# A two-layer encoder trunk with four token mixers: the S5 mixer's steps come first, not last, in the list that interleaves the mixers

## The chip, the cores and the metric

One core of a Trainium2 chip runs the whole program. The metric is device time in microseconds (us) from the start to the end of one execution; the time of the kernel before is the median of three executions. Engines are named as in the profile: PE (TensorE's matmuls), PEld (its weight loads), DVE (VectorE), ACT (ScalarE), POOL (GpSimd) and SP (SyncE, which here only issues DMAs).

## What is computed

The input is one sequence of 512 frames of width 1024, in float32. Each of two layers does this (cut to what matters):

```python
h = x @ w_in[l]                      # projections for four mixers
o_ret = retention(rq, rk, rv, rg)    # branch 0
o_att = chunk_attention(aq, ak, av)  # branch 1
o_gla = gla(gq, gk, gv, gr, ga)      # branch 2
o_s5  = s5(su, ...)                  # branch 3
mixed = sum(sigmoid(x @ w_gate[l, b] + b_gate[l, b]) * (o[b] @ w_branch[l, b]) for b in range(4))
x = layer_norm(ALPHA * x + mixed @ w_out[l])
ffn = (silu(x @ w_ffn_gate[l]) * (x @ w_ffn_up[l])) @ w_ffn_down[l]
x = layer_norm(ALPHA * x + ffn)
```

S5 is a complex diagonal linear recurrence over the 512 frames, 16 groups of 16 channels with 64 states each, followed by a GELU and a sigmoid gate. The four mixers do not depend on each other. Each needs only its own projections of x, and the merge needs all four.

## The kernel before, in words

Every large product is made as three passes in a 32-bit format of PE, on a high and a low half of each operand. The halves of a weight block are made on the chip: ACT casts the block (`wh<-wr`), DVE subtracts (`wl<-wr,wh`). So each 1024x128 block of weights costs PE 48 matmuls of 256 columns, ACT one cast and DVE one subtraction. `wr` has two buffers, `wh` and `wl` three.

A layer has five stages: projections; the stage of the mixers, with the gates between them; the output projection with a layer norm; the FFN's first products; the FFN's last product with a layer norm. Only the mixers' stage concerns us. In it stand, as Python generators that yield between their steps:

- `attention` (tiles `as` scores, `pp` probabilities, `at` transposed, `ao` output), four heads;
- `ret()`, which makes retention's projections (`rq`, `rk`, `rg`) and then runs `retention` (`rs`, `ro`, `rn`), the latter only once one half of attention's output is there;
- `gl()`, which makes GLA's projections (`gn`, `gq`, `gr`) once attention is done, and runs `gla` (`ga`, `gz`, `gu`, `go`) once one half of retention's output is there;
- `s5`, eight steps j = 0 to 7 and a gated end (`sg`). A step has a pair of matmuls for its inputs (`sv<-stk,sbs`), six products on DVE, two scans on DVE (`sm<-mag,sm`), six more products, two splits into halves (`xrh`/`xrl`, `xih`/`xil`), and, one step later, six matmuls that add its part to the output (`sy<-xrh,cpd`). The multiplying tables `er`, `ei` of a step are made on POOL in layer 0 (six operations on 128x512) and loaded by DMA in layer 1. The input `stk` of step j+1 is cast on ACT (`prepare`) after the states of step j;
- `gate_stream`, the filler: 32 gates (`pg`, 48 matmuls each) and 32 branch products (`pb`, 6 matmuls each). At most seven gates may wait for their branch (`CAP`), and a branch product needs the branch's mixer to be done. The order of branches is attention, retention, GLA, S5.

What sets the order is `run`. It keeps a model of each engine's clock (`Pace`: a cost for every operation, a time at which each tile is ready). At every turn it asks each generator, in the order of its list, whether its next step is ready by the model's time of PE, and takes the first that is. If none is, it takes the one that is ready soonest. The filler stands last in that list. S5 yields twice per step with `spare`, which says "not ready before the model's DVE clock is less than 3 us ahead of the model's PE clock":

```python
live = [[g, next(g)] for g in (*gens, fill)]
...
now = [i for i in ok if at[i] <= pace.at["T"]]
i = now[0] if now else min(ok, key=lambda j: at[j])
...
return lambda: max(pace.at["V"] - SPARE, pace.ready(need))
```

The order in which steps are taken is the order in which instructions are written. The tile framework then orders each engine's instructions by a schedule of its own, near to that. Every engine works its list strictly in order at run time. Buffers: 53 slots of 128x512 floats for everything in the stage, and in PSUM five banks for the mixers' tiles and three for gates and branch products.

Of the kernel before, what the change touches and what calls it, by code (L numbers as in the profile page):

```python
# [132 lines left out]
def trunk_kernel(ctx: ExitStack, tc: tile.TileContext, xn, xt, wt, w2, wbr, wo, wgu, wdn,  # L133
# [23 lines left out]
    def slot(s, dt=F32, tag="a"):  # L157
        n = nm(s)
        return ap_.tile([P, 512], dt, tag=tag, name=n, bufs=BUFS[tag])
# [13 lines left out]
    def split(h, l, src):  # L173
        A.copy(h, src)
        V.tensor_tensor(l, src, h.bitcast(F32), ALU.subtract)

    def split_slots(s, src, tags=("a", "a")):
        h, l = slot(s + "h", F32R, tags[0]), slot(s + "l", F32R, tags[1])
        split(h, l, src)
        return h, l  # L180
# [154 lines left out]
    def gemm_t(src, s, late=None):  # L335

        return gemm_ts([src], s, late)[0]
# [16 lines left out]
    def gemm_n(srcs, width, pre=None, late=None):  # L354

        pss = [mm_ps("gn") for _ in range(3)] + [mx_ps("gn")]
        ws = []

        def prod(c, t):
            h, l = ws[c]  # L360
            for kk in range(2):
                k = 2 * c + kk
                for j, (xx, w) in enumerate(((XH, h), (XL, h), (XH, l))):
                    T.matmul(pss[t][:, :width], xx[:, k, P * t:P * t + P],
                             w[:, kk * width:(kk + 1) * width],
                             start=(k == 0 and j == 0), stop=(k == 7 and j == 2))

        for c in range(4):
            ws.append(wload(srcs[c], 2 * width, 2, lambda i: pre(2 * c + i)) if pre else
                      wload(srcs[c], 2 * width))  # L370
            if late and c == 2:
                late()
            for t in range(3 if late and c < 3 else 4):
                prod(c, t)
            if late and c == 2:
                for c_ in range(3):
                    prod(c_, 3)
        return pss
# [108 lines left out]
    def silu_of(ps):  # L487

        t, s = slot("st"), slot("sg")
        A.activation(t, ps, AF.Tanh, scale=0.5)  # L490
        V.scalar_tensor_tensor(s, t, 1.0, ps, ALU.add, ALU.mult)
        return s
# [84 lines left out]
    def rotary(ps, ctab, stab, order):  # L577
        f = slot("rf")
        A.copy(f, ps)
        yield [f, ctab, stab]  # L580
        sw = mx_ps("rs")
        T.matmul(sw, perm, f, start=True, stop=True)
        a, b = slot("ra"), slot("rb")
        V.tensor_tensor(b, sw, stab, ALU.mult)
        V.tensor_tensor(a, f, ctab, ALU.mult)
        V.tensor_tensor(a, a, b, ALU.add)
        return spread(split_slots("rq", a), order)

    def spread(hl, order):

        x = dr.tile([3, P, 512], F32, name=nm("spr"))
        for i in range(3):
            SP.dma_start(x[i], hl[order[i]].bitcast(F32))
        return x
# [75 lines left out]
    def gla_in(pss):  # L670

        gk, gv = slot("gk"), []
        ga = sm.tile([P, 4, 32], F32, tag="ga", name=nm("ga"))
        G.memset(ga[:, :, 16:32], 1.0)
        for t in range(4):
            A.copy(gk[:, P * t:P * t + P], pss[t][:, 0:P])
            A.copy(ga[:, t, 0:16], pss[t][:, 384:400])
            g = slot("gv", F32R)
            split(g[:, 0:256], g[:, 256:512], pss[t][:, 128:384])
            gv.append(g)  # L680
        return gk, ga, gv
# [298 lines left out]
    def run(fill, *gens):  # L980


        live = [[g, next(g)] for g in (*gens, fill)]
        while live:
            at = [pace.ready(x[1]) for x in live]
            ok = [i for i, t in enumerate(at) if t is not None]
            now = [i for i in ok if at[i] <= pace.at["T"]]
            i = now[0] if now else min(ok, key=lambda j: at[j])
            try:
                live[i][1] = next(live[i][0])  # L990
            except StopIteration:
                live.pop(i)
# [9 lines left out]
    for l in range(L):  # L1002
        tt_ = lambda i, s: gemm_t(wt[l, i], s)

        pv = gemm_n(w2[l, 0], 512, load_x if l == 0 else None, rest)
        vr, va = [], []
        for t in range(4):
            for c, v in enumerate((vr, va)):
                x = slot("v", F32R)
                split(x[:, 0:256], x[:, 256:512], pv[t][:, 256 * c:256 * c + 256])  # L1010
                v.append((x[:, 0:256], x[:, 256:512]))
        uspr = []
        for i in range(2):
            ps = tt_(11 + i, "su")
            uspr.append(spread(split_slots("u", ps), (0, 1, 0)))
        if l == 0:
            SP.dma_start(ct, cst)
            SP.dma_start(pt, par)
            G.tensor_scalar(hb, pt[:, :, 0:36], 0.5, None, ALU.mult)
            s5c = s5_constants(0)  # L1020
        aq = [split_slots("aq", tt_(4 + i, "aq")) for i in range(2)]
        ak = [split_slots("ak", tt_(6 + i, "ak")) for i in range(2)]
        if l > 0:
            rows()
            with tc.issue_after(wdma[0].ins):
                for t in range(4):
                    for h in range(2):
                        SP.dma_start(xsp[P * t:P * t + P, 512 * h:512 * h + 512], xh[t][h])
        brs = [[None, None] for _ in range(4)]
        mix = []  # L1030
        rd = {}

        def ret():
            tabs = []
            for i in range(4):
                tabs.append(slot("rot"))
                SP.dma_start(tabs[i], rot[i])
            yield ()
            q = yield from rotary(tt_(0, "rq"), *tabs[0:2], (0, 1, 0))
            yield ()  # L1040
            k = yield from rotary(tt_(1, "rk"), *tabs[2:4], (0, 0, 1))
            g = []
            for i in range(2):
                yield ()
                g.append(silu_of(tt_(2 + i, "rg")))
            yield lambda: None if brs[1][0] is None else 0.0
            yield from retention(q, k, vr, g, brs[0])

        def gl():
            yield lambda: None if brs[1][1] is None else 0.0  # L1050
            kv = gla_in(gemm_n(w2[l, 1], 400))
            yield ()
            gq = slot("gq")
            A.activation(gq, tt_(8, "gq"), AF.Copy, scale=32.0 ** -0.5)
            g = []
            for i in range(2):
                yield ()
                g.append(silu_of(tt_(9 + i, "gr")))
            yield lambda: None if brs[0][0] is None else 0.0
            yield from gla(l, *kv, gq, g, brs[2])  # L1060

        g_gate = gate_stream(l, (1, 0, 2, 3), brs, mix)
        run(g_gate, attention(l, aq, ak, va, brs[1]), ret(), gl(), s5(l, s5c, uspr, brs[3]))
        xh = [[slot("x") for _ in range(2)] for _ in range(4)]
        for t in range(4):
            for h in range(2):
                src = xn if l == 0 else xsp
                SP.dma_start(xh[t][h], src[P * t:P * t + P, 512 * h:512 * h + 512])
        gt, bt = ln_params(l, 0)
        rest, rows = proj_ln(l, 0, [m[0] for m in mix], [m[1] for m in mix], 8, wo[l], 4, 2, xh, gt, bt, False)  # L1070


        gt, bt = ln_params(l, 1)
        ghs, gls = [], []
        ps = gemm_ts([wgu[l, i] for i in range(3)], "pg", rest)
        for f in range(NF):
            if f > 0:
                ps += [gemm_t(wgu[l, i], "pg") for i in range(max(3, 2 * f), 2 * f + 2)]
            pg, pu = ps[2 * f:2 * f + 2]
            if f == 1:  # L1080
                rows()
            s = slot("fs")
            A.activation(s, pg, AF.Silu)
            V.tensor_tensor(s, s, pu, ALU.mult)
            h, l_ = split_slots("g", s, ("acc", "acc") if f < 4 else ("sg", "sg") if f < 7 else ("a", "a"))
            ghs.append(h)
            gls.append(l_)
            if l + 1 < L and f == 0:
                s5c = s5_constants(l + 1)
            if l + 1 < L and f % 2 == 0 and 4 <= f < 20:  # L1090
                j = f // 2 - 2
                for i, x in enumerate(s5_table(j, s5c[3])):
                    SP.dma_start(esp[j, i], x)
        rest, rows = proj_ln(l, 1, ghs, gls, NF, wdn[l], 4, 2, xh, gt, bt, l == L - 1)
# [140 lines left out]
```

## Time and profile before

| | us |
|---|---|
| median of three executions | 1720.33 (1717.82 to 1720.64) |
| the profiled execution's own time | 1720.08 |
| its span, first to last instruction | 1717.9 |
| PE busy | 1651.2 (96%) |
| PE weight loads busy | 1531.0 (89%) |
| DVE busy | 1000.2 (58%) |
| ACT busy | 613.4 (36%) |
| POOL busy | 353.4 (21%) |
| mixers' stage, layer 0 (first `as` to first `pj`) | 63.9 to 453.9 = 390.0 |
| mixers' stage, layer 1 | 927.9 to 1297.4 = 369.5 |

PE is busy nearly always, but "busy" also counts matmuls at half clock; the granted clock beside each window tells how much of that there is (1.00 is 2.4 GHz, and a mean of 0.94 over a window means that 12% of it went at 1.2 GHz). The time that the program could lose or win in a stage is therefore the stage's length against PE's work in it at full clock. DVE's 58% is a mean of very unlike stages; a window for each part of the mixers' stage tells more.

### The profile page before, as it was taken

The page shows a single profiled execution, that of the slowest core. Times are in us where ns is not written, and L with a number is a line of the kernel's source. Part 1 is how long each engine was busy: PE and PEld are TensorE (multiplying, and loading weights), DVE is VectorE, ACT ScalarE, POOL GpSimd, SP SyncE. Part 2 cuts the span into 40 slices and gives each one's busy share as a digit, 9 for nine tenths or more (in the row PEclk, how much of TensorE's full clock was granted, in tenths as well). Part 3 has the DMA queues.
Part 4 walks back from the last instruction along what each step waited for, and adds up shares of the span by engine and source line. Part 5 has one row for each costly group of instructions (what it writes and reads, how often), then busy time and mean ns, then how long its engine had stood idle before and what let it go on. Part 6 is the DMA issues. An engine that isn't in the chain of part 4 may idle for free. (4 is left out here: it accounts for less than half of the span.)

```text
span 1717.9 us, 27806 instructions
## 1 busy us (share of the span) xinstructions
PE 1651.2 (96%) x11596; PEld 1531.0 (89%) x11596; DVE 1000.2 (58%) x1473; ACT 613.4 (36%) x1012; POOL 353.4 (21%) x363
## 2 busy tenths in 40 slices
PE   8999998889999999999999999999999999999997
PEld 7989898779889999988889898988898899999886
DVE  4666579987586533322374665789865833333226
ACT  4454532233343222221154545433342522222112
POOL 0601024560038921000060000122300600000002
PEclk9998999899999999999999999999999999999999
DMA  6532212222433333322327332233324232222232
GB/s 200 176 111 76 86 62 94 82 82 99 141 99 99 123 123 117 119 98 98 111 74 259 104 96 92 64 117 125 125 93 160 86 102 96 99 99 99 98 99 74
DMA packets 66205, 186.94 MB, mean 109 GB/s; under 512 B 7136, under 2 KB 7328, under 8 KB 66080
## 3 DMA queue, kind: packets, MB, share of 16 engines
q1 hardware_dynamic: 66080, 185.17, 32.7%
q8 instruction: 91, 1.49, 0.4%
q14 instruction: 34, 0.28, 0.0%
HBM read 170.46 MB, written 14.68 MB: 108 GB/s over the span
## 5 line engine op out<-in xcount | busy, mean ns | idle before, releaser
L121 DVE TENSOR_TENSOR wl<-wr,wh 128x1024 fp32r<-128x1024 f32 (+2 forms) x250 | 317.3, 1270 | 440.9 <-ACT wh L121 427.0
L121 ACT CAST wh<-wr 128x1024 fp32r<-128x1024 f32 (+2 forms) x250 | 257.5, 1032 | 671.1 <-PE pg L121 223.6
L121 PE MATMUL pg<-XH,wh 128*128 128x256 f32 x2432 | 337.4, 281 | 2.2 <-DVE fs L121 2.2
L121 PE MATMUL pg<-XL,wh 128*128 128x256 f32 x2432 | 333.8, 280 | 2.5 <-DVE XL L121 2.5
L121 PE MATMUL pg<-XH,wl 128*128 128x256 f32 x2432 | 333.0, 280 | 0.0
L121 PEld LDWEIGHTS pg<-XH,wh 128*128 128x128 f32 x2432 | 312.1, 192 | 8.1 <-issue 3.1
L121 PEld LDWEIGHTS pg<-XL,wh 128*128 128x128 f32 x2432 | 306.0, 191 | 3.3 <-DVE XL L121 3.3
L121 PEld LDWEIGHTS pg<-XH,wl 128*128 128x128 f32 x2432 | 305.9, 191 | 0.4
L121 POOL TENSOR_TENSOR rs<-ve,ct 128x1 f32<-128x1 f32 x16 | 10.9, 682 | 718.2 <-DVE ve L121 718.2
L121 DVE TENSOR_TENSOR fs<-fs,pg 128x512 f32<-128x512 f32 x44 | 30.2, 687 | 159.5 <-PE pg L121 159.5
L121 PE MATMUL pj<-wl,gh 128*128 128x512 f32 x320 | 102.3, 393 | 0.0
L121 PE MATMUL pj<-wh,gl 128*128 128x512 f32 x320 | 101.8, 391 | 0.0
L121 PE MATMUL pj<-wh,gh 128*128 128x512 f32 x320 | 101.7, 391 | 0.0
L121 POOL TENSOR_TENSOR acc<-acc,sg 128x512 f32<-128x512 f32 x32 | 61.6, 1929 | 170.3 <-DVE sg L121 170.3
L121 PEld LDWEIGHTS pj<-wh,gh 128*128 128x128 f32 x320 | 59.9, 188 | 13.5
L121 PEld LDWEIGHTS pj<-wl,gh 128*128 128x128 f32 x320 | 60.1, 188 | 13.1
L121 PEld LDWEIGHTS pj<-wh,gl 128*128 128x128 f32 x320 | 60.1, 188 | 12.7
L121 PE MATMUL gn<-wh,XH 128*128 128x400 f32 (+1 forms) x128 | 49.1, 384 | 6.2 <-ACT XH L121 6.2
L121 POOL TENSOR_TENSOR hr<-hv,ct 128x8 f32<-128x8 f32 x8 | 13.2, 1648 | 192.0 <-DVE hv L121 192.0
L121 PE MATMUL pb<-brh,bwh 128*128 128x512 f32 x128 | 51.8, 404 | 0.0
L121 PE MATMUL pb<-brh,bwl 128*128 128x512 f32 x128 | 51.3, 401 | 0.0
L121 PE MATMUL pb<-brl,bwh 128*128 128x512 f32 x128 | 51.3, 401 | 0.0
(320 smaller groups left out, 2584.0 us busy)
## 6 DMA issues: line engine op xcount, KB each, us to landing
wr<-in_wt SPq DMA_DIRECT2D x90, 512.0 KB
wr<-in_wgu SPq DMA_DIRECT2D x88, 512.0 KB
wr<-in_wdn SPq DMA_DIRECT2D x44, 512.0 KB
bwr<-in_wbr SPq DMA_DIRECT2D x32, 256.0 KB
wr<-in_wo SPq DMA_DIRECT2D x16, 512.0 KB
skr<-spr SPq DMA_DIRECT2D x32, 192.0 KB
wr<-in_w2b SPq DMA_DIRECT2D x8, 400.0 KB
wr<-in_w2a SPq DMA_DIRECT2D x8, 256.0 KB
```

Of the source, the lines that this page charges most:

```text
L121: r = fn(out, *a, **kw)
```

## The change: what it does

One line. S5's generator moves from the last to the first place among the four mixers in the list of `run`; the filler still comes last.

```diff
         g_gate = gate_stream(l, (1, 0, 2, 3), brs, mix)
-        run(g_gate, attention(l, aq, ak, va, brs[1]), ret(), gl(), s5(l, s5c, uspr, brs[3]))
+        run(g_gate, s5(l, s5c, uspr, brs[3]), attention(l, aq, ak, va, brs[1]), ret(), gl())
```

No instruction is added or removed; both programs hold the same matmuls, the same DVE, ACT and POOL operations and the same DMAs. What moves is the order on every engine, from the start of the mixers' stage to its end, in both layers.

In the three places that follow, neighbouring rows that only repeat are left out. On PE in layer 0, the second pair of S5's input products (`sv`, the step j = 1). Before, it stands behind GLA's last output products (`go`) and the eleventh gate, 1295 matmuls into the stage:

```order
L121 MATMUL go_2934<-gsh_2858,qh_2324 128x256
L121 MATMUL go_2934<-gsl_2859,qh_2324 128x256
L121 MATMUL go_2934<-gsh_2858,ql_2325 128x256
L121 MATMUL pg_2974<-XH,wl_2970 128x256 x8
L121 MATMUL sv_3029<-stk_2546,sbs_902 128x512
L121 MATMUL sv_3031<-stk_2546,sbs_902 128x512
L121 MATMUL pb_3057<-brh_2275,bwh_2480 128x512
```

With the change it stands 561 matmuls into the stage, between two heads of attention:

```order
L121 MATMUL pg_1653<-XL,wh_1648 128x256 x8
L121 MATMUL pg_1653<-XH,wl_1649 128x256 x8
L121 MATMUL sv_1708<-stk_1563,sbs_794 128x512
L121 MATMUL sv_1710<-stk_1563,sbs_794 128x512
L121 MATMUL ao_1292<-pth_1570,v_271 128x128
L121 MATMUL ao_1292<-ptl_1571,v_271 128x128
L121 MATMUL at_1742<-ct,pp_1380 128x128
```

Steps 1 to 7 thus moved out of the last third of the stage into attention, retention and GLA, and gates that stood ahead of them now stand behind them.

On PE in layer 0, the end of S5. Before, S5's last `sy` group is followed by 4 gates, the 12 `sg` products and 8 branch products up to the first output projection. With the change the last `sy` group (here broken up by a gate) is followed by more than 13 gates and 15 branch products, the first of them still GLA's:

```order
L121 MATMUL pg_3975<-XL,wh_3970 128x256 x4
L121 MATMUL sy_2998<-xrl_3782,cpd_3683 128x512
L121 MATMUL sy_2998<-xih_3785,cpd_3683 128x512
L121 MATMUL sy_2998<-xil_3786,cpd_3683 128x512
L121 MATMUL pg_3975<-XH,wl_3971 128x256 x8
L121 MATMUL pb_4054<-brh_3620,bwh_3679 128x512
L121 MATMUL sg_4026<-ygh_2682,swgh_3895 128x512
L121 MATMUL pg_4141<-XH,wh_4136 128x256 x8
```

What moved here is nearly ten gates and seven branch products, from ahead of S5's last step to behind it.

On ACT in layer 0, the casts around the input of S5's step 7. Before, the cast of the second state half (`xih`) of step 6, the next step's input (`stk`) behind it, and only weights and gates around them:

```order
L121 CAST wh_4547<-wr_4546 128x1024
L121 ACTIVATE sg_4371<-pg_4322,hb 128x512
L121 CAST xih_4293<-sm_4200 128x512
L121 CAST stk_4305<-skr_4208 96x512
L121 CAST cpd_4384<-scc_771 128x2x32
```

With the change the same pair, with GLA's and retention's norms (`hq`), states (`gsh`) and outputs (`brh`) ahead and behind:

```order
L121 CAST gsh_3367<-gs_3354 128x512
L121 CAST brh_3435<-hf_3433 128x512
L121 ACTIVATE hq_3513<-go_3509 128x512
L121 CAST xrh_3586<-sm_3180 128x512
L121 CAST xih_3590<-sm_3182 128x512
L121 CAST stk_3602<-skr_3190 96x512
L121 CAST brh_3620<-hf_3618 128x512
```

The pair itself did not move apart: `stk` of a step still stands right behind `xih` of the step before. What stands around it now belongs to the other mixers.

## Rows read from the trace of the kernel before

**Rows 1.** The page's head: the span, and each engine's busy time.
```profile
span 1717.9 us, 27806 instructions
...
PE 1651.2 (96%) x11596; PEld 1531.0 (89%) x11596; DVE 1000.2 (58%) x1473; ACT 613.4 (36%) x1012; POOL 353.4 (21%) x363
```

**Rows 2.** Windows of the mixers' stage: length, each engine's busy time (instructions), PE's clock, DMA.
```profile
63.90:253.00 189.10, 182.92 (x1308) 169.57 (x1308) 127.63 (x250) 92.60 (x191) 32.60 (x38) 0.97 0.30 99
253.00:416.20 163.20, 139.76 (x972) 131.60 (x971) 149.20 (x171) 48.70 (x77) 82.34 (x58) 0.94 0.27 87
416.20:453.90 37.70, 37.70 (x261) 35.04 (x260) 25.55 (x36) 16.53 (x25) 0.00 (x0) 1.00 0.19 65
63.90:453.90 390.00, 360.38 (x2536) 336.21 (x2536) 302.38 (x457) 157.83 (x291) 114.94 (x95) 0.96 0.28 91
927.90:1113.40 185.50, 181.21 (x1307) 168.29 (x1307) 121.28 (x250) 92.54 (x191) 13.83 (x16) 0.98 0.33 106
1113.40:1259.70 146.30, 135.37 (x972) 127.89 (x971) 130.02 (x171) 49.06 (x77) 32.43 (x22) 0.97 0.38 118
1259.70:1297.40 37.70, 37.70 (x260) 35.06 (x259) 25.53 (x36) 16.55 (x25) 0.00 (x0) 1.00 0.19 65
927.90:1297.40 369.50, 354.27 (x2535) 331.23 (x2535) 276.82 (x457) 158.16 (x291) 46.26 (x37) 0.98 0.33 107
```

**Rows 3.** PE's waits over the whole span: us in total, times, longest.
```profile
PE sv L121 <- ACT stk L121: 19.1, 6, 6.2
PE sv L121 <- DVE sbs L121: 13.7, 4, 4.2
...
PE rs L121 <- DVE ptl L121: 5.7, 5, 1.6
PE hn L121 <- DVE ro L121: 3.2, 2, 1.7
...
PE sv L121 <- ACT bwh L121: 1.6, 1, 1.6
```

**Rows 4.** Timeline of layer 0 between two S5 steps: start, us, engine, operation [idle before, releaser].
```profile
301.09 1.54 DVE L121 TENSOR_TENSOR sm<-sm,er 128x512 f32<-128x512 f32 x1
...
302.73 0.62 ACT L121 CAST xih<-sm 128x512 fp32r<-128x512 f32 x1 [4.44 <-DVE sm L121]
303.25 0.61 ACT L121 CAST stk<-skr 96x512 fp32r<-96x512 f32 x1
303.38 0.71 DVE L121 TENSOR_TENSOR xil<-sm,xih 128x512 fp32r<-128x512 f32 x1 [0.74 <-ACT xih L121]
...
303.92 0.79 PE L121 MATMUL sv<-stk,sbs 96*128 96x512 f32 x1 [6.16 <-ACT stk L121]
```

**Rows 5.** SP's waits in layer 0's mixers' stage.
```profile
SPq L121 <- DVE wl L121: 294.4, 37, 13.4
```

**Rows 6.** Windows of S5's own instructions (tile sm): length, DVE, ACT busy, clock, DMA.
```profile
63.90:453.90 390.00, 109.38 (x128) 9.92 (x16) 0.96 0.28 91
927.90:1297.40 369.50, 97.89 (x128) 9.94 (x16) 0.98 0.33 107
```

**Rows 7.** The same for the weights' low halves (tile wl): PE, PEld, DVE busy.
```profile
63.90:453.90 390.00, 98.89 (x657) 86.69 (x656) 58.98 (x44) 0.96 0.28 91
927.90:1297.40 369.50, 98.09 (x657) 85.97 (x656) 52.86 (x44) 0.98 0.33 107
```

**Rows 8.** PE's timeline in layer 0: eight gate matmuls a row, then branch products.
```profile
309.69 1.07 PE L121 MATMUL pg<-XH,wl 128*128 128x256 f32 x8
310.60 1.07 PE L121 MATMUL pg<-XH,wh 128*128 128x256 f32 x8
...
314.71 0.39 PE L121 MATMUL pb<-brh,bwh 128*128 128x512 f32 x1
314.93 0.39 PE L121 MATMUL pb<-brl,bwh 128*128 128x512 f32 x1
```

## The prediction

> **What bounds the kernel now.** I read the page's head first [rows 1]: PE is busy 96% of 1717.9 us, so a change that only moves work can win where PE waits or runs at half clock, or lose by making it wait more. The change touches the mixers' stages alone, 390.0 and 369.5 us; the rest I leave as it is.
>
> Next the windows of these stages, cut where S5's step 1 begins and where S5's last output product ends [rows 2]. The reader should see three unlike parts. In the first (189.1 and 185.5 us) DVE is busy 67% and 65%, and PE sets the pace. In the second, S5's steps 1 to 7, DVE is busy 149.2 of 163.2 us in layer 0 and 130.0 of 146.3 in layer 1. There PE's busy time, less what went at half clock (length times one minus the clock), is 139.8 - 9.8 = 130 and 135.4 - 4.4 = 131 us. So the second part lasts 14.0 us longer than the busier engine (DVE) needs in layer 0 and 15.3 us longer than PE needs in layer 1. Over seven steps that is 2.0 and 2.2 us a step. The third part (37.7 us) has PE busy throughout at full clock.
>
> Third, PE's waits [rows 3]: 19.1 + 13.7 + 1.6 = 34.4 us end with S5's input products `sv`. The timeline [rows 4] shows the link behind them: DVE ends the last product of a step's states at 302.6, ACT casts `xih`, then the next step's `stk` behind it, and only then, at 303.92, may PE start `sv`, after 6.16 us of idle time.
>
> **The change, part by part.** Nothing is added or removed, so it is a matter of balance: how much PE work and how much DVE work stand between two marks in the new order. I cut it into head (first scores to `sv` of step 2), middle (to the last `sy` of step 7) and tail (to the first `pj`).
>
> Prices for PE: a gate matmul starts 0.91/8 = 0.1135 us after the one before, a 512-column one 0.23 us [rows 8]; for the 400-column `gn` I take 0.18 between them. A stage holds 346 us of PE work at full clock (360.4 - 15.6 and 354.3 - 7.4, mean) [rows 2]. Of its 2536 matmuls 1872 are of the gate's kind (212.5 us), 252 of the `pb`, `sy`, `sg` kind (58 us), 96 `gn` (17 us); the other 316 share the remaining 58 us, 0.18 each.
> Prices for DVE: a step of S5 is an eighth of 109.4 us in layer 0 and of 97.9 in layer 1, 13.7 and 12.2 [rows 6]. A weight's low half is 58.98/44 = 1.34 and 52.86/44 = 1.20 [rows 7]. The other 285 instructions share what is left of 302.4 and 276.8 [rows 2], 0.47 and 0.44 each.
>
> Tail: 656 gate matmuls (74.5 us) and 102 of 512 columns (23.5 us), 98 us, with 61 DVE instructions beside them. PE sets its pace, as in the third part today, with no loss.
> Middle: the order of the change holds 688 (layer 1: 733) matmuls of the gate's kind, 138 (144) of 512 columns, 58 (96) `gn` and 173 (180) others: 78.1 + 31.7 + 10.4 + 31.1 = 151 us, and 83.2 + 33.1 + 17.3 + 32.4 = 166 us. On DVE: six steps of S5, 18 (19) weights, 133 (135) others: 82.0 + 24.1 + 62.5 = 169 us and 73.4 + 22.8 + 59.7 = 156 us. So DVE sets the pace in layer 0, and PE, barely, in layer 1.
> Head: what remains of 346, 97 and 82 us of PE. Today's first part loses 11.9 and 8.0 us to waits and half clock (its length less 177.2 and 177.5 us of PE work); by the head's share of that work, 6.5 and 3.7 us.
>
> Links: 2.1 us for each of the six steps of the middle, 12.6 us a layer, as today. Below that lies nothing (another mixer's work fills DVE during the link); above, the next term.
> Lumps: the middle is not even. Between the `sy` of step 5 and that of step 7 the new order has 160 gate matmuls, 66 of 512 columns and 29 others, 38.6 us of PE; on DVE two steps of S5, six weights and 60 others, 63.5 us in layer 0 and 58.2 in layer 1. If neither engine can work ahead across that mark, the middle is the rest (112.7 and 127.4 us, PE) plus the lump, 176.2 and 185.6 us, not 168.6 and 166.0: 27.2 us more in both layers. If it works ahead freely, nothing more. I take half, 13.6.
> Banks: the five PSUM banks now serve S5 and the others at once. In the built orders, a bank is written again within 5 us of PE work after its last use 16 times before, 37 times now, both layers. Today's waits of this kind, `rs` and `hn`, are 8.9 us for 16 [rows 3], 0.56 each; 21 more are 11.7 us. Many will fall where PE waits anyway: from 0 to 11.7, I take half, 5.9.
> Costed at nothing: S5's loads, moved among the weights of attention's time on SP, which idles 294.4 us of layer 0's stage waiting for a free weight buffer [rows 5]; that cover would be gone only if a load waited more than the 8 us that such a wait lasts on average. POOL makes the tables earlier in layer 0; it is busy 114.9 of 390 us [rows 2], and what it costs DVE is in layer 0's higher prices. Behind ACT's `xih` now stand attention's casts, not only weights; a late `xih` delays them, which is the lumps' term again.
>
> Sum: layer 0, 96.7 + 6.5 + 168.6 + 12.6 + 98 = 382.4; layer 1, 82 + 3.7 + 166 + 12.6 + 98 = 362.3. Together 744.7 against 759.5, 14.8 less; with lumps and banks, 4.7 us more. On the profiled execution, 1720.08, that is 1724.8; the median of the runs lies 0.25 higher. I forecast **1725**.
>
> Row and rule: the windows [rows 2] show DVE at 67% and then 91% of layer 0's first two parts. The Trainium skill (Perfetto Trace Analysis, Optimization Strategy) says that where the most-contended engine changes over time, interleaving those regimes may help. The trace agrees that there are two regimes here; by the rule alone the sum would stay at 14.8 us less or go below it, by the uneven order it does not.
>
> **The rivals.**
> *The two regimes do fill each other.* Attention's and retention's DVE work is independent of S5's, so DVE need not stand still during a link. For it: in today's first part DVE has a third of its time free [rows 2]. Against it: the lump, where everybody's DVE work comes at once. Without lumps and bank waits, and with half of the links covered, 14.8 + 12.6 = 27 us less: 1693.
> *The lump decides (slower).* The place is the end of the middle, retention's second norm, GLA's norms and S5's steps 6 and 7. Retention and GLA feed DVE only there, so it cannot work ahead, and the input of step 7 waits for `xih` of step 6 behind all of it. With the lump whole: -14.8 + 27.2 + 5.9 = 18 us more, 1739. It decides from the point where DVE has not finished step 6's states when PE reaches `sv` of step 7. For it: each link in today's trace is this same chain [rows 4]. Against it: DVE is ahead of PE before the lump in layer 1.
> *Buffers run short.* If each of the 21 new tight bank writes waits as long as the longest `rs` wait, 1.7 us [rows 3], 36 us come in place of 5.9: 35 us more, 1755. The Trainium skill (the same section) says that the same gap repeating can mean that SBUF or PSUM is too small for the next tile. Today's `rs` waits are few and short, so the trace bears it out little.
> *It does not do what it says.* The planner could choose nearly the old order, whatever the list; the new order shows S5 moved by hundreds of matmuls, so hardly: 1720.
>
> **How the numbers follow.** My forecast has 0.42, the regimes filling each other 0.30, the lump 0.16, buffers 0.10, no effect 0.02. A measurement of this kernel can tell 0.2%, 3.4 us, from no change. The forecast's own range is 1712 to 1736; of its chance I put 0.06 below -0.2%, 0.14 within, 0.22 above. So faster 0.36, same 0.16, slower 0.48. The signs are close, and 0.2% lies inside the bounds of one term. The range leaves out half of the fast rival's far end and most of the buffers': 1698 to 1752.
>
> **What would show it.** Right: a tail of about 98 us with PE at clock 1.00, 60 us longer than today's third part; a middle of 180 to 190 us with DVE over 88% busy in layer 0; waits at `sv` for `stk` of 25 us or more, most at step 7; total length of the two stages near 764 us. Wrong: a middle of 170 us or less in both layers (the regimes fill each other), or waits of `rs`, `at`, `ro` and `as` on DVE that sum to over 25 us (banks), or waits of gates on their weights, which would mean that SP's queue, costed at nothing, was held up.

## The result, and the profile after

| | before | after |
|---|---|---|
| median, us | 1720.49 (1717.82 to 1721.45, 4 executions) | 1735.62 (1731.62 to 1747.56, 4) |
| profiled execution, us | 1720.08, span 1717.9 | 1731.62, span 1729.8 |
| mixers' stage, layer 0 | 390.0 | 65.3 to 456.9 = 391.6 |
| mixers' stage, layer 1 | 369.5 | 929.7 to 1309.4 = 379.7 |

The ratio is 1.0095, with a 95% interval of 1.0071 to 1.0120: slower. Now and then an execution runs long at a lower granted clock, as one of the six of the fastest run below did (1804.01 us at 0.854); the medians in this document count such executions, the ratios and their intervals do not. The profiled executions differ by 11.9 us of span, and the two stages by 1.6 + 10.2 = 11.8 us, so all of it lies there. How it splits between the layers is less sure, as the runs with one layer alone will show. The page's head of the changed kernel, which answers to [rows 1]:

```profile
span 1729.8 us, 27901 instructions
...
PE 1661.7 (96%) x11596; PEld 1524.7 (88%) x11596; DVE 983.5 (57%) x1473; ACT 610.0 (35%) x1012; POOL 337.7 (20%) x363
```

PE has the same 11596 matmuls and is busy 10.5 us longer (1651.2 us before). The windows of the mixers' stages of the changed kernel, cut as the prediction cut them (first scores, `sv` of step 2, last `sy`, first `pj`), with the columns of [rows 2]; each layer's last line is its whole stage:

```profile
65.30:164.00 98.70, 96.98 (x712) 88.28 (x711) 79.78 (x151) 49.03 (x105) 32.05 (x36) 1.00 0.37 120
164.00:354.30 190.30, 165.30 (x1067) 145.47 (x1067) 162.20 (x250) 73.12 (x139) 62.83 (x51) 0.95 0.24 76
354.30:456.90 102.60, 101.42 (x761) 96.51 (x760) 46.87 (x57) 34.67 (x48) 10.90 (x8) 1.00 0.27 89
65.30:456.90 391.60, 363.70 (x2536) 330.26 (x2536) 288.85 (x457) 156.82 (x291) 105.77 (x93) 0.97 0.28 90
929.70:1018.00 88.30, 85.69 (x616) 77.58 (x616) 69.11 (x139) 44.56 (x97) 5.38 (x8) 0.96 0.44 141
1018.00:1207.20 189.20, 174.54 (x1163) 157.42 (x1163) 155.92 (x262) 76.43 (x147) 23.81 (x22) 0.97 0.31 95
1207.20:1309.40 102.20, 101.27 (x760) 96.38 (x759) 46.75 (x57) 34.68 (x48) 10.87 (x8) 1.00 0.28 89
929.70:1309.40 379.70, 361.50 (x2535) 331.38 (x2535) 271.78 (x457) 155.67 (x291) 40.06 (x37) 0.98 0.33 104
```

Against the stage lines of [rows 2], PE's time outside its busy time went from 29.6 + 15.2 = 44.9 to 27.9 + 18.2 = 46.1 us. So the waits were exchanged almost one for one, and the other 10.5 us are the same matmuls taking longer. The clock is not the reason: its mean over the run rose from 0.983 to 0.988. Which waits came in place of the old ones, the view of PE's waits tells, which answers to [rows 3]:

```profile
PE hn L121 <- DVE go L121: 11.0, 4, 3.5
...
PE go L121 <- DVE go L121: 4.8, 2, 2.4
PE hn L121 <- DVE ro L121: 3.7, 4, 1.5
PE sy L121 <- DVE xrl L121: 3.4, 2, 1.7
```

No row of `sv` is left; 34.4 us of them stood in [rows 3]. In their place stand waits of GLA's end (`hn` and `go` on DVE's `go`, 15.8 us; the kernel before has no row with these releasers) and of S5's outputs (`sy`, 7.8 us in four rows, the largest shown). The timeline of the place in layer 1, with the columns of [rows 4], shows GLA's norm going from engine to engine while PE has little to do:

```profile
1156.12 0.68 DVE L121 TENSOR_REDUCE hm<-go 128x8 f32<-128x512 f32 x1
...
1159.04 0.68 DVE L121 SCALAR_TENSOR_TENSOR go<-hm,go 128x512 f32<-128x512 f32 x1
...
1159.76 0.63 ACT L121 ACTIVATE hq<-go 128x512 f32<-128x512 f32 x1 [1.85 <-DVE go L121]
...
1159.87 0.35 PE L121 MATMUL go<-gsh,qh 128*128 128x256 f32 x1 [2.42 <-DVE go L121]
...
1160.58 0.68 DVE L121 TENSOR_REDUCE hv<-hq 128x8 f32<-128x512 f32 x1
...
1161.87 1.64 POOL L121 TENSOR_TENSOR hr<-hv,ct 128x8 f32<-128x8 f32 x1 [6.79 <-DVE hv L121]
1163.54 0.69 DVE L121 TENSOR_TENSOR go<-go,hr 128x512 f32<-128x512 f32 x1 [1.49 <-POOL hr L121]
...
1164.29 1.11 PE L121 MATMUL hn<-ct,go 128*128 128x128 f32 x4 [3.47 <-DVE go L121]
...
1169.90 0.63 PE L121 MATMUL pb<-brl,bwh 128*128 128x512 f32 x1
...
1173.22 0.39 PE L121 MATMUL pb<-brh,bwh 128*128 128x512 f32 x1
```

From the reduction to the transposition (`hn`) 8.2 us pass, on DVE, ACT, DVE, POOL and DVE, with S5's products among them on DVE (left out here). The reader should look for a gate here and find none. They should also see the branch products behind the wait take 0.63 us, and 0.39 from about 1172 us on, at 1.2 and then 2.4 GHz. The window around it (columns of [rows 2]), and then PE's busy time for GLA's `go` in each stage, 4.89 and 4.90 us in the kernel before:

```profile
1153.20:1178.00 24.80, 16.73 (x64) 11.86 (x64) 18.41 (x34) 4.67 (x8) 8.20 (x6) 0.79 0.18 53
```

```profile
65.30:456.90 391.60, 7.47 (x32) 0.97 0.28 90
929.70:1309.40 379.70, 7.03 (x32) 0.98 0.33 104
```

With `gu` (4.5 to 9.2 us) and `hn` (4.6 to 6.6) GLA's own products take 11.5 us more in both layers together. They are not alone: `sy`, `gn` and `pb` take 12.3 us more, `sv`, `rs` and `pg` 4.3 us less (busy times of tiles overlap, so these do not add up to the 10.5). A part of it is how busy time is counted: a product that no other follows at once counts for its whole length (0.35 us for the 256 columns of `go` above), where eight in a row start 0.91/8 us apart [rows 8]. How large that part is was not measured. Before, by the built order, two gates a layer stood between the first `go` and the last `hn`; now 0.6.

The theory from these rows: the 32 gates of a layer are a fixed stock of PE work that needs nothing but weights. They are the cover under which the mixers' serial chains cross DVE, ACT and POOL. Asked for first, S5 runs beside attention and retention, the gates beside it are written until seven wait for their branch, and GLA's end finds none. 13.7 gates are left for the tail, where they cover nothing.

### The profile page after: what moved, and what is told of

Read it like the earlier page. It is cut to its first block, busy times and chain, and to the rows that moved or that the text cites. A ratio compares the mean times of both kernels' runs of the same rounds, so it can differ in the third digit from the quotient of the medians.

```text
span 1729.8 us, 27901 instructions
## 1 busy us (share of the span) xinstructions
PE 1661.7 (96%) x11596; PEld 1524.7 (88%) x11596; DVE 983.5 (57%) x1473; ACT 610.0 (35%) x1012; POOL 337.7 (20%) x363
## 4 chain that ended last, share of the span: by engine, by line
PE 40%; issue 20%; DVE 6%; POOL 2%; ACT 1%; DMA 1%; DVEq 0%; SPq 0%; POOLq 0%; ACTq 0%
PE pg L121 21%; PE pj L121 9%; PE gn L121 2%; DVE sm L121 2%; PE pb L121 2%; POOL x L121 1%; DVE wl L121 1%; PE rg L121 1%; PE su L121 1%; PE ak L121 1%; PE aq L121 1%; DVE x L121 1%; DVE s5w L121 1%; PE gr L121 1%; PE as L121 1%
## 5 line engine op out<-in xcount | busy, mean ns | idle before, releaser
L121 PEld LDWEIGHTS pg<-XH,wh 128*128 128x128 f32 x2432 | 307.2, 188 | 8.0 <-issue 3.4
L121 PEld LDWEIGHTS pg<-XL,wh 128*128 128x128 f32 x2432 | 302.5, 188 | 4.1 <-DVE XL L121 3.3
L121 POOL TENSOR_TENSOR acc<-acc,sg 128x512 f32<-128x512 f32 x32 | 46.8, 1471 | 143.6 <-DVE sg L121 143.4
L121 PEld LDWEIGHTS pj<-wl,gh 128*128 128x128 f32 x320 | 60.1, 188 | 13.1
L121 POOL MEMSET cpd<- 128x512 f32 x16 | 8.6, 535 | 249.5 <-PE ao L121 61.8
```

What stands on the lines that cost most here:

```text
L121: r = fn(out, *a, **kw)
```

## The experiments

The kernel before had medians of 1720.3 to 1721.6 us beside these runs.

**S5 first in one layer only** (the other keeps it last).

```diff
+        s5_, at_ = s5(l, s5c, uspr, brs[3]), attention(l, aq, ak, va, brs[1])
+        if l in (0,):
+            run(g_gate, s5_, at_, ret(), gl())
+        else:
+            run(g_gate, at_, ret(), gl(), s5_)
```

> S5 first in layer 0 alone, last in layer 1. In the profiles layer 0's stage of the mixers grew by 1.6 us and layer 1's by 10.2. Theory (DVE's work bunches where few gates stand beside it; layer 0's stage was already limited by DVE before, layer 1's was not): 0 to 5 us over the kernel before, and layer 1's stage at 369 to 371 us. Rival (PSUM banks and buffers are shared by more mixers at once, the same in both layers): about half of the whole loss, 6 to 9 us over.

> S5 first in layer 1 alone. Theory: 8 to 14 us over the kernel before, layer 0's stage at 389 to 391 us. Rival (buffers): 6 to 9 us over, as in layer 0 alone. If both single layers sum to the whole change (about 15 us), the two stages are independent.

Layer 0: 1727.92, ratio 1.0028 (0.9997 to 1.0058), unclear: the medians lie 6.5 us apart, inside the rival's 6 to 9, and the ratio stands for 4.8 us, inside the theory's 0 to 5; its 12 executions go from 1719 to 1736. Layer 1: 1734.26, ratio 1.0066 (1.0042 to 1.0091), 12.9 us by the medians, as the theory had it. The two ratios sum to 1.0094, the whole change's 1.0095, so the layers act independently as far as the noise tells. A single profiled stage is a rough guide, though. The stage left alone, with its order unchanged, took 366.5 us in the first run's profile (layer 1) and 394.0 in the second's (layer 0), 3.0 below and 4.0 above the kernel before, both outside what was expected. So the 1.6 and 10.2 us above are no split to rely on.

**Does the amount of DVE work set the pace?** Each of S5's two scans a step becomes one product, so the recurrence is left out (in both orders).

```diff
-            V.tensor_tensor_scan(m2, mg, m1, 0.0, ALU.mult, ALU.add)
+            V.tensor_tensor(m2, mg, m1, ALU.mult)
```

> The changed kernel with S5's two scans of a step replaced by one product each, so the recurrence is left out; the order of PE and ACT is the same instruction by instruction. A scan pair holds DVE 3.3 us, a pair of products 1.2 to 1.4, so DVE has about 2 us less to do in each step, 16 us less a layer at most, and 4 us less between the last output products of steps 5 and 7. Theory (DVE limits the middle of the stage): 14 to 26 us below the changed kernel (1710 to 1722). Rival (banks and buffers limit it): under 6 us below. Rival (PE at half clock is the loss, not DVE): under 6 us below, at the same granted clock.

> The kernel before with the same products in place of scans (recurrence left out), same order of PE and ACT. Theory: S5's steps 1 to 7 are limited by DVE in layer 0 and by the link between steps in both; 12 to 24 us below the kernel before (1697 to 1709), waits at the sv products down from 34 us to under 15. Rival (the waits at sv come from the link's fixed hops, not from DVE's amount of work): under 6 us below, waits at sv over 25 us.

S5 first: 1729.14, 6.5 us below the changed kernel, between the theory's 14 to 26 and the rivals' under 6. S5 last: 1706.44, ratio 0.9916 (0.9884 to 0.9948), 15 us below the kernel before, as the theory had it, though the waits at `sv` fell only to 22.7 us, not under 15. The edit took less off DVE than was expected, since a scan in the changed kernel takes 1.22 us on average, not half of 3.3: DVE is busy 280.5 and 263.5 us in the two stages, 16.6 us less than in the changed kernel, and with S5 last 295.1 and 269.8, 14.3 us less than in the kernel before. So in the old order the time fell by as much as DVE's work did, and in the new by less than half of it. DVE's amount alone does not set the new middle's length; that it sets none of it is not shown, and the two gains, 6.5 and 15 us, differ by little more than the noise (each ratio's interval is 4 to 6 us either way). With less work on DVE the waits of GLA's end are where they were (PE's waits, S5 first):

```profile
PE hn L121 <- DVE go L121: 10.5, 4, 3.5
PE go L121 <- DVE go L121: 4.8, 2, 2.4
```

**Fewer gates in the middle**, more behind the last `sy`. `held` is 12 from the start of a stage and 32 once GLA is written.

```diff
-            more = ng < len(todo) and ng - nb < CAP
+            more = ng < held[0] and ng - nb < CAP
```

> The changed order, but the filler may write only 12 gates until GLA's last product is written. In the built order this moves 3.3 gates a layer (18 us of PE work at full clock) from S5's and GLA's middle to behind the last sy: 17.0 gates stand there and not 13.7, and none is left between GLA's first state product and its first output product (1.5 in the changed kernel). Theory (the middle lasts as long as the chains of GLA and S5, and gates are the only cover of their waits): the middle gets shorter by less than 8 us a layer while the tail grows by 18, so the time rises by 20 to 36 us, to 1755 to 1772, with PE's waits at hn, go and gu longer. Rival (PE's work sets the middle's length, gates or not): what the tail gains the middle loses, and the time stays within 5 us of the changed kernel's 1735.6.

1761.59, ratio 1.0229 (1.0197 to 1.0262). From the first scores to the last `sy` the stage went from 289.0 to 281.3 us and from 277.5 to 264.4, the tail from 102.6 and 102.2 to 126.3: of 23.7 and 24.1 us moved away 7.7 and 13.1 came back (the second is more than the 8 expected). The time lies in the theory's range and far from the rival's. The waits of `go` went from 5.9 to 18.2 us and those of `gu` from 1.0 to 5.9, as expected; those of `hn` did not grow (14.7 and 12.3). A window of GLA's end in layer 1 (columns as above) shows what PE did without gates:

```profile
1150.00:1185.00 35.00, 21.23 (x78) 16.12 (x79) 29.71 (x56) 7.05 (x12) 6.88 (x5) 0.56 0.08 25
```

PE has 78 matmuls in 35 us, at a mean clock of 0.56; DVE is busy 85%.

**S5 second, S5 third** (the edit shown is the second place; for the third, S5 stands between `ret()` and `gl()`).

```diff
-        run(g_gate, s5(l, s5c, uspr, brs[3]), attention(l, aq, ak, va, brs[1]), ret(), gl())
+        run(g_gate, attention(l, aq, ak, va, brs[1]), s5(l, s5c, uspr, brs[3]), ret(), gl())
```

> S5 is asked for second, behind attention and ahead of retention and GLA. In the built order 2.8 gates stand between GLA's first output product and its last transposition (0.6 with S5 first, 2.0 with S5 last), and 10.0 behind the last sy (13.7 and 4.0). Theory (gates missing beside GLA's end cost the changed kernel some 13 us a layer there): half or more of it is won back, so 1708 to 1724, faster than the changed kernel and about the time of the kernel before. Rival (the cost grows with how far S5's steps are moved ahead): a value between the two kernels, 1727 to 1732, with the waits at go and hn as in the changed kernel, over 10 us.

> S5 is asked for third, behind attention and retention and ahead of GLA alone. 4.0 gates stand between GLA's first output product and its last transposition, 7.0 behind the last sy. Theory: GLA's end is covered as in the kernel before or better, while some of S5's links find GLA's work beside them: 1705 to 1718, below the kernel before. Rival (distance moved): 1721 to 1727.

Second: 1744.50, ratio 1.0134 (1.0097 to 1.0170), slower than either kernel, which neither expectation had. Third: 1729.53, ratio 1.0014 (0.9982 to 1.0046), no difference that can be told, and above both ranges expected. So more gates at GLA's end alone win nothing. PE's waits with S5 second:

```profile
PE sy L121 <- ACT xrh L121: 14.1, 5, 6.5
PE hn L121 <- DVE go L121: 4.4, 2, 2.2
```

GLA's wait is down from 11.0 to 4.4 us, as expected of its gates; S5's outputs in the steps behind it now wait instead, and 77 us of tail, ten gates among it, still follow. With S5 third the waits are those of `sv` again (18.9 on `sbs`, 7.0 on `stk`). Each time one chain is covered, another waits; with ten gates left, a used-up stock does not explain why S5's outputs wait.

**S5 last, with the planner's price of a scan mended**, and then also with six gates kept back until S5's last output product is written (`held` 26).

```diff
+        if name == "tensor_tensor_scan":
+            return 0.068 + n * 3.17e-3
```

> The kernel before (S5 last), but the planner's model prices a scan at 0.068 + 512 x 0.00317 = 1.69 us and not at 0.60, near what the trace shows. This asks whether S5's place matters through the planner's wrong picture of DVE's clock. Expected by the theory that the old order's waits at sv come from a planner that thinks DVE ahead: the planner puts more gates before each step, sv waits fall below 20 us from 34, and the time falls by 5 to 15 us, to 1706 to 1716. By the rival (sv's waits are the hop through ACT, which no price of scans changes, and the built order leaves no gate behind the last sy where 4 stood): no gain, 1718 to 1735.

> S5 last with the scans priced at 1.69 us, and six of the 32 gates kept back until S5's last output product is written. In the built order three gates stand behind the last sy, where none stood without the keeping back (and waits of 16.3 us at sy and 11.1 us at sg, both layers together, followed). Theory (gates as cover): the waits at sg go and those at sy shrink to below 8 us, sv's stay below 20; the time falls by 12 to 25 us from 1734, to 1709 to 1722. Rival (the gates that are kept back are missing elsewhere as much): 1728 to 1738, with the waits at sv back above 25 us.

Priced: 1734.22, ratio 1.0093 (1.0063 to 1.0123), the rival's range and no gain. Kept back: 1748.04, ratio 1.0162 (1.0127 to 1.0198), above even the rival's 1728 to 1738. PE's waits, priced:

```profile
PE sy L123 <- ACT xrh L123: 16.3, 2, 8.1
PE sg L123 <- ACT swgh L123: 11.1, 2, 5.6
PE sv L123 <- ACT stk L123: 7.0, 2, 5.4
...
PE sv L123 <- DVE sbs L123: 4.2, 1, 4.2
```

and with gates kept back:

```profile
PE sy L123 <- ACT xrh L123: 27.0, 6, 8.0
PE sg L123 <- ACT swgh L123: 11.1, 2, 5.6
```

With the price, `sv` waits 12.8 us in all (1.6 of them on `bwh`) instead of 34.4, as the theory said, and S5's end pays for the gates spent on it. Keeping some back left `sv` at 9.6 us and made the waits of `sy` longer: the gates were missing in the steps ahead of that end; `sg`'s wait did not move, since on PE it stands ahead of the gates that were kept.

**More gates in the middle with S5 first**: the same price, and nine gates may wait.

```diff
-BUFS = {"a": 53, "sg": 7, "acc": 8}
+BUFS = {"a": 51, "sg": 9, "acc": 8}
-CAP = 7
+CAP = 9
+        if name == "tensor_tensor_scan":
+            return 0.068 + n * 3.17e-3
```

> S5 first, with more gates in the middle: the planner prices a scan at 1.69 us, and 9 gates may wait for their branch, not 7 (two slots for tiles go to them). In the built order 10.0 gates stand behind the last sy, 13.7 in the changed kernel; 3.0 (1.5) stand between GLA's first state product and its first output product, and 1.1 (0.6) from there to its last transposition. It is the mirror of the run with fewer gates in the middle: 3.7 gates, 20 us of PE work a layer, go back. Theory (gates are the cover of chains that set the middle's length): the middle grows by less than 12 us a layer and the tail falls by about 20, so the time falls by 12 to 30 us to 1705 to 1723, the kernel before or below. Rival (PE's work sets the middle): what the tail loses the middle gains, 1730 to 1740.

1722.82, ratio 1.0025 (0.9997 to 1.0053): 12.8 us below the changed kernel, at the edge of what the theory allowed; price and buffers were changed together. By layers it is half right. In both, the tail shrank by 24 us, to 78. The part before it grew by 13.7 us in layer 1, but by 24.0 in layer 0, where nothing was won.

**S5 first, at a slower pace**: the price of the scans, buffers as in the changed kernel, and S5's steps held to 2 and then 1.5 us of DVE's lead.

```diff
-SPARE = 3.0
+SPARE = 1.5
+        if name == "tensor_tensor_scan":
+            return 0.068 + n * 3.17e-3
```

> S5 first, scans priced at 1.69 us, and S5's steps may be taken when the model's DVE clock is less than 2 us (not 3) ahead of PE's; buffers as in the changed kernel. In the built order 7.0 gates (layer 0) and 5.0 (layer 1) stand behind the last sy, 13.7 in the changed kernel and 10.0 in the run with more gates in the middle; 3.0 and 2.8 stand between GLA's first state product and its first output product, 1.9 and 1.8 from there to its last transposition. Theory (gates left behind the last sy cover nothing; each one brought forward to a chain that waits pays): below 1720, 1702 to 1718, so the kernel before is beaten or met. Rival (the run with more gates in the middle won by its buffers, not by the place of the gates): 1725 to 1740.

> The same with 1.5 us. Now 2.0 and 1.0 gates stand behind the last sy, 1.1 and 1.0 between GLA's first state product and its first output product, 2.9 and 3.0 behind that. Theory: the stock of gates is spent too early, S5's own end has too little beside it, and waits at sy and sg appear as in the run with S5 last and priced scans (27 us there): slower than with 2 us, 1712 to 1735. Rival (fewer gates left behind is always better): faster than with 2 us, below 1705.

With 2 us: 1702.87, ratio 0.9893 (0.9857 to 0.9929), as the theory said. With 1.5 us: **1687.37, ratio 0.9788 (0.9750 to 0.9825)**, the fastest of all, and by far below what the theory gave it. The theory expected S5's end to stay without cover, as with S5 last; the rival, that fewer gates left behind are always better, was right on the time. The head and PE's waits of the last run:

```profile
span 1680.9 us, 27843 instructions
...
PE 1641.2 (98%) x11596; PEld 1516.6 (90%) x11596; DVE 995.1 (59%) x1473; ACT 610.0 (36%) x1012; POOL 346.3 (21%) x363
```

```profile
PE hn L123 <- DVE ro L123: 3.7, 3, 1.5
...
PE hn L123 <- DVE go L123: 1.7, 1, 1.7
PE sv L123 <- ACT stk L123: 1.5, 1, 1.5
...
PE sg L123 <- ACT swgh L123: 0.9, 1, 0.9
```

No wait of `sy` is left, and those of `go`, `sv` and `sg` are small. PE's time outside its busy time in the two stages is 18.6 us, where it was 44.9 and 46.1. Quarters of layer 0's stage show what else differs (length, then PE, PEld, DVE, ACT, POOL busy, clock, DMA): before, after, and this run.

```profile
63.90:161.40 97.50, 93.20 (x639) 84.88 (x639) 72.11 (x146) 48.53 (x108) 23.45 (x28) 0.95 0.34 113
161.40:258.90 97.50, 95.62 (x714) 90.20 (x713) 61.12 (x110) 44.97 (x84) 15.05 (x14) 1.00 0.26 81
258.90:356.40 97.50, 81.03 (x552) 75.74 (x551) 89.50 (x100) 30.03 (x47) 48.18 (x34) 0.93 0.25 83
356.40:453.90 97.50, 90.53 (x637) 85.39 (x637) 79.66 (x103) 34.31 (x52) 28.26 (x20) 0.97 0.26 85
```

```profile
65.30:163.00 97.70, 95.98 (x706) 87.49 (x706) 79.06 (x148) 48.03 (x102) 31.05 (x35) 1.00 0.38 121
163.00:261.00 98.00, 86.01 (x552) 76.78 (x551) 85.44 (x133) 39.98 (x85) 35.92 (x32) 0.95 0.28 88
261.00:359.00 98.00, 84.99 (x560) 74.01 (x559) 79.56 (x123) 35.39 (x59) 28.65 (x20) 0.95 0.22 67
359.00:456.90 97.90, 96.72 (x725) 91.99 (x724) 44.79 (x55) 33.42 (x47) 10.16 (x7) 1.00 0.26 85
```

```profile
63.70:153.00 89.30, 88.05 (x663) 80.78 (x663) 71.47 (x140) 46.11 (x101) 30.08 (x33) 1.00 0.38 126
153.00:243.00 90.00, 85.04 (x550) 77.91 (x549) 72.79 (x121) 42.75 (x89) 23.77 (x21) 0.97 0.25 84
243.00:333.00 90.00, 88.04 (x645) 82.23 (x645) 74.35 (x101) 31.99 (x48) 36.49 (x26) 0.99 0.27 89
333.00:421.80 88.80, 85.14 (x624) 79.70 (x624) 71.52 (x85) 31.35 (x48) 22.46 (x15) 1.00 0.28 95
```

DVE's share by quarters is 74, 63, 92 and 82% with S5 last; 81, 87, 81 and 46% with S5 first; and 80, 81, 83 and 81% at the slower pace (73, 70, 82 and 81% in its layer 1). An even share is not enough by itself: with S5 second it is 74, 78, 86 and 60%, and third 73, 70, 89 and 76%, both somewhat more even than with S5 last, and neither is faster. At the slower pace four of S5's steps stand ahead of GLA's first `go` and four behind it (in layer 1 three and five; with S5 last one and seven), and two gates in layer 0, one in layer 1, stand between the last `sy` and `sg`. (The stage is not shorter by all that its windows show: the first `pj` now comes ahead of the last gate and two branch products. The span tells the gain, 37.0 us.) The price, 1.69 us, lies above what a scan takes on average: 1.50 in the kernel before, 1.22 in the changed one, 1.47 here. The two edits of these runs were not tried apart, nor was the slower pace with S5 last: what each is worth alone stays open, and so does which of the differences above brings the gain.

## Why the prediction was right in number and where its steps failed

The forecast was 1725 us with a range of 1698 to 1752, and slower as the likeliest sign; 1735.6 lies inside, 10.6 above the forecast. The time rose by 15.1 us where 4.7 was forecast, and several terms came out right for other reasons than the prediction gave.

- **Cut and balance.** Head 98.7 and 88.3 us (forecast 103.2 and 85.7), middle 190.3 and 189.2 (188.0 and 191.4, with links, half of each layer's lump and half of the banks): right in length.
- **Tail: the term that was mis-sized.** 98 us was forecast; 102.6 and 102.2 it is, 8.8 us in both layers and more than the whole error of the sum (771.3 measured, 764.2 forecast). That it is PE-bound at clock 1.00 was right. The price of a gate's matmul was taken from one pair of rows, 0.1135 us [rows 8]; in the tail most rows of eight start 0.94 or 0.95 us apart, and the mean is about 0.118 us a matmul (two rows of layer 1's):

```profile
1241.42 1.11 PE L121 MATMUL pg<-XL,wh 128*128 128x256 f32 x8
1242.37 1.11 PE L121 MATMUL pg<-XH,wl 128*128 128x256 f32 x8
```

  Over 656 matmuls that is some 3 of the 4.6 us in layer 0; in another 1.2 us PE was not busy, which the prediction put at nothing ("with no loss").
- **DVE sets the middle's pace in layer 0: wrong.** Its amount was forecast at 169 and 156 us, measured at 162.2 and 155.9. But it is busy 85 and 82% there, not over 88, and lighter scans gave back 6.5 us for 16.6 us of DVE's work. A step of S5 also became cheaper on DVE in layer 0, 94.64/8 = 11.8 us against 13.7 [rows 6]; the scans, 46.9 us in all before and 38.8 now, are a part of it:

```profile
65.30:456.90 391.60, 94.64 (x128) 9.66 (x16) 0.97 0.28 90
```

- **Links: wrong in place.** 25 us or more at `sv` for `stk`, most at step 7, were forecast; none came. The waits of GLA's norms and S5's outputs, 15.8 + 7.8 = 23.6 us, came to nearly the same sum as the two times 12.6 forecast. That is luck: the size was carried over from the old order, and it was the size of another wait.
- **Lumps: right that they cost, wrong in why.** Between the `sy` of step 5 and that of step 7 pass 54.6 and 54.0 us, for 38.6 of PE's work: 16.0 and 15.4 lost. But DVE is busy only 43.3 us there in either layer, where 63.5 and 58.2 were forecast: 66 of its instructions fall there and not 98, and their amount does not fill the time. What ends the waits there is GLA's norm (`hn` and `go` on DVE's `go`, 8.2 and 7.6 us). The rival of the lump named that place, and its 1739 is the nearest of all to the measured time, but the condition it rested on, step 7's input waiting for `xih`, did not occur.
- **Banks: not borne out.** The waits of `rs`, `at`, `ro` and `as` on DVE sum to 6.5 us (25 was the mark), and to 6.5 in the kernel before (5.7 of `rs` [rows 3] and 0.8 of `at`). No gate waits for its weights, so SP was rightly costed at nothing.
- **The rival of 1693, regimes that fill each other,** did not come with this change; the slower pace, with its new price, gives 1687. The Trainium skill (Perfetto Trace Analysis, Optimization Strategy) says that interleaving such regimes may help. The best run's trace agrees (DVE's share 80 to 83% in each of layer 0's quarters, 2.1% faster); the changed kernel's does not: moved whole, the unequal parts only change places, the light one from the second quarter (63%) to the last (46%), and the time rose.
- **What the prediction lacked** is the stock of gates. It counted them as PE work that may stand anywhere; where they stand decides which chain is covered. The run with fewer gates in the middle shows this most directly; S5 second and the gates kept back, both slower than expected, show that a count of gates by place does not yet give the time.

Open remain why layer 0 won nothing from more gates, why S5 second is the worst of the four places, and how much of PE's longer busy time in the changed kernel comes from gates that are missing.

## What to carry to other kernels

Work that depends on weights alone is the cover of work that waits, and it is finite: before a priority is changed, count where the filler will stand in the new order, chain by chain, and how much of it is left at the end, where it hides nothing. When one wait goes and the time does not, look in the same view for the next chain. And with a list of priorities, try the pace (how far ahead one generator may run) together with the place: first at the old pace cost 0.95%, first at half the lead, with a higher price for its scans, won 2.1%.

## What the runs showed of the hardware that was not expected

A wait cost more than its length here. The granted clock fell during the 3.47 us wait of `hn` in layer 1, and PE's products ran at 1.2 GHz until about 1172 us, 7.7 us after the wait ended: 0.63 us for a branch product, 0.39 then. In the mean of 35 us without gates the clock was 0.56. The best run has a mean clock of 0.996 against 0.983 of the kernel before and PE busy 10.0 us less for the same 11596 matmuls (1641.2 and 1651.2), beside the waits that it saves. But the clock does not rank the kernels: the changed one, at 0.988, is slower than the one before.

S5's scan (`sm<-mag,sm`, 128x512) took 1.2 us or nearly twice that. In the kernel before, nine of the 32 take 1.9 to 2.3 us, and beside each of the nine POOL is at work for 1.16 us or more; beside the 23 others, of 1.19 to 1.22 us, it is for 1.06 at most. With S5 first hardly any POOL work falls beside them, and all 32 take 1.20 to 1.23 us. That POOL's work is the reason was not tried by itself.
